# Attention weights of a hybrid streaming encoder: transposes by DMA instead of TensorE

## The chip, the core and the metric

One program on one core of a Trainium2 chip. The core has five engines, each with an instruction queue of its own that runs in order: TensorE (PE; its weight loads are listed apart as PEld), VectorE (DVE), ScalarE (ACT), GpSimd (POOL) and SyncE (SP), which here issues nearly all DMAs. Matrix products land in PSUM (eight banks of 128 x 512 f32); SBUF holds the rest. The metric is the device time of one execution in microseconds (us): the median before the change is 2810.27 us over three runs (2809.77 to 2811.77).

## The reference

One layer on x[1, 2048, 1024] in f32: a root-mean-square norm, one input projection whose columns feed three groups of heads (a diagonal state-space layer, differential attention with 6 heads, a gated linear recurrence called HGRN2), an output projection with residual, then a gated MLP with a causal convolution, and a last norm. The change lies in the attention:

```python
def attend(args):                      # one block of 128 queries
    q_blk, blk = args
    sc = jnp.einsum('bqhcd,bkhcd->bhcqk', q_blk, k).astype(jnp.float32) * scale
    ...
    bias = jnp.where(visible[None], -slopes[:, None, None] * dist[None], MASK_VALUE)
    p = jax.nn.softmax(sc + bias[None, :, None], axis=-1)
    w = p[:, :, 0] - lam * p[:, :, 1]
    return jnp.einsum('bhqk,bkhd->bqhd', w, v)
```

Each head has two softmax maps (c = 0, 1) that are joined into one matrix of weights w, which multiplies the values; each head's output is then normed. A block of queries sees the keys up to its own end.

## The kernel before

Products are made in f16 with values split in two: a high half, f16(a), and a low half, f16(a - high); three products (high high, high low, low high) stand for an f32 one.

The program is written as two streams of Python generators. `left` makes the projections and then the attention; `right` makes the state-space layer, HGRN2, the output projection and the MLP. `weave` joins them by weights, and a list scheduler with a timing model then sets the order of instructions on each engine at build time. On the chip each engine runs that order and waits on semaphores. SP's DMAs too go out in that order: a DMA that waits for an engine holds those behind it.

`phase_attn` runs twice: for query blocks 0 to 7 (keys up to 1024), and in its `lean` form for blocks 8 to 15 (keys up to 2048), each time over six heads, 96 blocks in all. One block i of a head, with L = 128 (i + 1) keys:

- Scores (L835): for both maps, products of 512 keys each into a PSUM tile t_ps (two buffers). DVE adds the distance bias and writes to t_sc, one f32 tile [128 queries, keys] for each map, with a running maximum t_mx (L839). t_sc has six buffers in the first form, four in the lean one, so three and two blocks in flight.
- t_nm, the exponents' offset (L844); exponentials by ACT in place with their sums t_la (L849); a ratio t_a (L854, L855); then DVE joins the maps in place, in pieces of 1024 keys (L861): t_sc[0] = t_sc[1] * t_a + t_sc[0].
- To the keys' side (L871 to L875): for each 512 keys, four f32 transposes on PE into the single PSUM buffer t_pt; ACT copies it twice, scaled by 16: as f32 to t_wf and as f16 to t_wt[:, 0]; POOL writes the difference to t_wt[:, 1].
- The product with the values (L883): for each 128 keys three matmuls of 64 columns into t_po, high high, high low, low high; ACT copies t_po to t_y and sums its squares (L887, L889).

After a head's eight blocks the norm's factors are made (L893 on, with a factor 1/16), and after every second head t_y is transposed through t_pt too (L910), split into t_yo and stored.

Beside the attention PE makes HGRN2's projections (g_pq, g_pv, both at L98) up to about 1000 us, a part of the output projection (o_pm, L1394), from 1225 us on the up products of the MLP's first half of the tokens (f_pm, L98), and at the end the first of its down products (f_pd, L1679). For half of the MLP's up weights, POOL makes sums (f_sum, L141), which ACT and DVE split into f_w (L54, L62), and SP stores them to Wd; the others are loaded from Wd (L150). After the attention come the second half's up products, and the down products of both.

Of the kernel before, what the change touches and what calls it, by code (L numbers as in the profile page):

```python
# [26 lines left out]
CH = 512  # L27
# [682 lines left out]
class AttnConst:  # L710


    def __init__(self, K, cp, lq1, lk1, lq2, lk2, subln_g):
        nc = K.nc
        V = nc.vector
        self.base = base = cp.tile([128, S], F32, name="t_base")
        nc.gpsimd.iota(base.bitcast(I32), pattern=[[-1, S]], base=S - 128, channel_multiplier=1)
        V.tensor_copy(base, base.bitcast(I32))
        V.scalar_tensor_tensor(
            out=base, in0=base, scalar=-1.0, in1=base, op0=ALU.mult, op1=ALU.min  # L720
        )
# [12 lines left out]
        self.nlam = nlam = cp.tile([128, 1], F32, name="t_nlam")
        V.tensor_tensor(out=nlam, in0=lexp[:, 1:2], in1=lexp[:, 0:1], op=ALU.subtract)
        V.tensor_scalar(out=nlam, in0=nlam, scalar1=-lam_init, scalar2=None, op0=ALU.add)
        self.lk = lk = cp.tile([128, 2], F32, name="t_lk")
        nc.gpsimd.memset(lk, 0.0)
        V.tensor_tensor(out=lk[:, 0:1], in0=lsum[:, 0:1], in1=lsum[:, 1:2], op=ALU.max)
        V.tensor_scalar(out=lk[:, 0:1], in0=lk[:, 0:1], scalar1=0.0, scalar2=None, op0=ALU.max)  # L740
        V.tensor_scalar(
            out=lk[:, 0:1], in0=lk[:, 0:1], scalar1=-1.0, scalar2=-math.log(2.0 + lam_init),
            op0=ALU.mult, op1=ALU.add,
        )
        self.gc = gc = cp.tile([128, 1], F32, name="t_gc")
        for e in range(2):
            nc.sync.dma_start(
                out=gc[64 * e:64 * e + 64, :], in_=subln_g[0].rearrange("(p o) -> p o", o=1)
            )
        V.tensor_scalar(  # L750
            out=gc, in0=gc, scalar1=(1.0 - lam_init) * YS, scalar2=None, op0=ALU.mult
        )


def phase_attn(K, A, QKd, Vd, Yd, i0, i1, s_bufs, lean):

    tc, nc = K.tc, K.nc  # L760
    V = nc.vector
    NT = i1 - i0
# [2 lines left out]
    with ExitStack() as es:  # L765
        kp = es.enter_context(tc.tile_pool(name="t_k", bufs=2, reuse_waits="tile"))
        sp = es.enter_context(tc.tile_pool(name="t_s", bufs=s_bufs, reuse_waits="tile"))
        wp = es.enter_context(tc.tile_pool(name="t_w", bufs=4 if lean else 5, reuse_waits="tile"))
        mp = es.enter_context(tc.tile_pool(name="t_m", bufs=3, reuse_waits="tile"))
        op = es.enter_context(tc.tile_pool(name="t_o", bufs=2, reuse_waits="tile"))  # L770
        ps_s = es.enter_context(tc.tile_pool(name="t_ps", bufs=2, reuse_waits="tile", space=PSUM))
        ps_t = es.enter_context(tc.tile_pool(name="t_pt", bufs=1, reuse_waits="tile", space=PSUM))
        ps_o = es.enter_context(tc.tile_pool(name="t_po", bufs=1, reuse_waits="tile", space=PSUM))
        fp = es.enter_context(tc.tile_pool(name="t_f", bufs=2 if lean else 3, reuse_waits="tile"))
        kq = {}

        def stack(a, i, parts, h, cols):
# [28 lines left out]
        for h in range(NH):  # L806
# [13 lines left out]
            for i in range(i0, i1):  # L820
# [27 lines left out]
                for c in range(2):  # L848
# [7 lines left out]
                    out=a[:, 1:2], in0=la[:, 0, n_:n_ + 1], scalar1=a[:, 0:1], scalar2=nlam[:, 0:1],  # L856
                    op0=ALU.mult, op1=ALU.mult,
                )
                for k0 in range(0, L, 1024):
                    k1 = min(L, k0 + 1024)  # L860
                    V.scalar_tensor_tensor(  # L861
                        out=sc[0][:, k0:k1], in0=sc[1][:, k0:k1], scalar=a[:, 1:2],
                        in1=sc[0][:, k0:k1], op0=ALU.mult, op1=ALU.add,
                    )
                wts = []
                for k in range(0, L, 512):
                    n = min(512, L - k)
                    wt = wp.tile([128, 2, 512], F16, tag="w", name="t_wt")
                    pt = ps_t.tile([128, 512], F32, tag="t", name="t_pt")
                    for b in range(0, n, 128):  # L870
                        nc.tensor.transpose(pt[:, b:b + 128], sc[0][:, k + b:k + b + 128], K.ident)  # L871
                    wf = fp.tile([128, 512], F32, tag="f", name="t_wf")
                    nc.scalar.activation(out=wf[:, 0:n], in_=pt[:, 0:n], func=AF.Copy, scale=16.0)  # L873
                    nc.scalar.activation(out=wt[:, 0, 0:n], in_=pt[:, 0:n], func=AF.Copy, scale=16.0)  # L874
                    nc.gpsimd.tensor_tensor(  # L875
                        out=wt[:, 1, 0:n], in0=wf[:, 0:n], in1=wt[:, 0, 0:n], op=ALU.subtract
                    )
                    wts.append(wt)
                po = ps_o.tile([128, HD], F32, tag="o", name="t_po")
                for b in range(i + 1):  # L880
                    cc = slice(128 * (b % 4), 128 * (b % 4) + 128)
                    for w, v in ((0, 0), (0, 1), (1, 0)):
                        nc.tensor.matmul(  # L883
                            out=po, lhsT=wts[b // 4][:, w, cc], rhs=vt[:, b, 64 * v:64 * v + 64],
                            start=(b == 0 and w + v == 0), stop=(b == i and w == 1),
                        )
                nc.scalar.copy(ot[:, n_, :], po)  # L887
                sq = mp.tile([128, HD], F32, tag="sq", name="t_sq")
                nc.scalar.activation(  # L889
# [2 lines left out]
                yield 2 * (i + 1) + 1  # L892
            s, v = [mp.tile([128, NT], F32, tag=f"e{j}", name=f"t_e{j}") for j in range(2)]  # L893
            V.reciprocal(out=s, in_=la[:, 0, :])
            V.tensor_scalar(out=s, in0=s, scalar1=1.0 / 16.0, scalar2=None, op0=ALU.mult)
            V.tensor_tensor(out=v, in0=s, in1=s, op=ALU.mult)
            V.tensor_tensor(out=v, in0=v, in1=ss, op=ALU.mult)
            V.tensor_scalar(
# [6 lines left out]
                op=ALU.mult,  # L905
            )
            for j in range(NT // 4 if e == 1 else 0):
                pt = ps_t.tile([128, 512], F32, tag="t", name="t_pt")
                for b in range(4):
                    nc.tensor.transpose(pt[:, 128 * b:128 * b + 128], y[:, 4 * j + b, :], K.ident)  # L910
                o = op.tile([128, 2, CH], F16, tag="yo", name="t_yo")
                K.split(o[:, 0, :], o[:, 1, :], pt, gc[:, 0:1])
                c0 = 128 * i0 + j * CH
                nc.sync.dma_start(out=Yd[2 + h // 2, :, :, c0:c0 + CH], in_=o)
# [413 lines left out]
def phase_tail(K, x, Xd, Yd, Ad, w_out, norm_g, W, conv_w, conv_b, w_down, final_g, out, es,  # L1328
# [472 lines left out]
    def activations(hc, half, pool, pm, few, st_n, w_n, a_n, behind):  # L1801

        wp, st = pool("f_w1", w_n), pool("f_st1", st_n)
        sm = pool("f_sm1", 2) if half == 0 else None
        tp, ap = pool("f_t1", 2), pool("f_a1", a_n)
        done = factors(ap, Ad[half])
        ts = [
# [217 lines left out]
```

## Time and profile before

| What | Value |
| --- | --- |
| Median of three runs | 2810.27 us |
| The profiled execution | 2806.09 us, its span 2804.4 us |
| Mean granted PE clock | 0.943 |
| The attention, first score to last product | 440 to about 1950 us |
| Transposes of the weights, PE | 816, 146.6 us |
| ACT's copies to t_wf | 240, 126.7 us (those to t_wt 127.1) |
| POOL's subtractions to t_wt | 240, 286.5 us |
| Joining of the maps, DVE | 144, 167.9 us |

A row of a group has the engine, operation, output <- inputs, shape and count, then the busy time in all, the mean of one in ns, and the idle time of the engine before it with what ended it. Instructions overlap on PE, so its busy time over the count is less than the mean.

### The profile page before, as it was taken

To read this page: it belongs to the slowest core of one execution; us is meant where nothing else is said; L and a number is where in the kernel's file an instruction comes from. 1 tells how busy PE (TensorE), PEld (TensorE's weight loads), DVE (VectorE), ACT (ScalarE), POOL (GpSimd) and SP (SyncE) were. 2 spreads that over 40 slices of the span, in tenths; PEclk is the share of its full clock that TensorE was granted. 3 is DMA by queue.
4 is the path that set the end of the run, shared out by engine and by line. 5 is a ranking of instruction groups with operands and counts; after the bars stand their busy time and mean duration, and the time that the engine had idled before them with its cause. 6 is when DMAs were issued, how large, how long until landed. Compare 5 with 4: busy or idle time off the path is not lost.

```text
span 2804.4 us, 44619 instructions
## 1 busy us (share of the span) xinstructions
PE 2528.7 (90%) x16254; PEld 1465.3 (52%) x16254; DVE 2008.0 (72%) x3904; ACT 1341.1 (48%) x2579; POOL 1347.2 (48%) x1191
## 2 busy tenths in 40 slices
PE   5998898989999998968898888879999999999998
PEld 3654546877777765444444444434444444444443
DVE  7566745788787887798888889885654855555565
ACT  5333344557665665676565456653134422222221
POOL 4788602334343443266566666642801444444180
PEclk8999998989989989989999999989999999999999
DMA  6675553232223225623444434357775655554733
GB/s 225 234 219 187 166 169 99 65 91 69 60 78 91 52 86 134 211 84 112 135 135 128 152 111 128 101 213 242 270 264 197 215 166 155 166 154 143 267 105 120
DMA packets 339500, 420.74 MB, mean 150 GB/s; under 512 B 61840, under 2 KB 217808, under 8 KB 338256
## 3 DMA queue, kind: packets, MB, share of 16 engines
q1 hardware_dynamic: 317104, 377.51, 42.8%
q10 hardware_dynamic: 22176, 40.38, 3.9%
q8 instruction: 128, 2.10, 0.3%
q14 instruction: 92, 0.75, 0.1%
HBM read 289.30 MB, written 127.93 MB: 149 GB/s over the span
## 4 chain that ended last, share of the span: by engine, by line
PE 41%; DVE 16%; issue 6%; ACT 4%; DMA 4%; POOL 4%; SPq 0%; ACTq 0%; DVEq 0%; POOLq 0%
PE f_pm L98 18%; PE f_pd L1679 10%; DVE t_sc L839 3%; PE o_pm L1394 3%; DVE t_sc L861 2%; PE g_pv L98 2%; PE g_pq L98 1%; ACT t_sc L849 1%; PE t_pt L871 1%; DVE f_t L1520 1%; PE t_ps L835 1%; DVE f_w L62 1%; DMA o_y<-Yd 1%; PE g_pl L1147 1%; PE t_po L883 1%
## 5 line engine op out<-in xcount | busy, mean ns | idle before, releaser
L98 PE MATMUL f_pm<-f_q,f_w 128*128 128x512 f16 x3696 | 857.8, 388 | 6.2 <-DVE rs_i L72 5.7
L98 PEld LDWEIGHTS <-f_w 128*128 128x128 f16 x3696 | 365.3, 100 | 493.7 <-issue 98.4
L875 POOL TENSOR_TENSOR t_wt<-t_wf,t_wt 128x512 f16<-128x512 f32 (+2 forms) x240 | 286.5, 1195 | 451.3 <-ACT t_wt L874 365.0
L1679 PE MATMUL f_pd<-f_dw,f_da 128*128 128x512 f16 x1848 | 406.9, 382 | 9.5 <-DMA f_da<-Ad 7.8
L1679 PEld LDWEIGHTS <-f_da 128*128 128x128 f16 x1848 | 181.3, 98 | 228.7 <-DMA f_da<-Ad 8.8
L849 ACT ACTIVATE t_sc<-t_sc,t_nm 128x128 f32<-128x128 f32 (+7 forms) x192 | 229.2, 1198 | 53.5 <-DVE t_nm L844 51.9
L835 PE MATMUL t_ps<-t_k,t_q 96*128 96x512 f16 (+2 forms) x480 | 170.0, 369 | 83.7 <-DVE t_mx L839 80.5
L839 DVE CUSTOM_DVE_ANT_0 t_sc<-t_ps,t_base,t_mx 128x512 f32<-128x512 f32 (+3 forms) x288 | 185.2, 643 | 36.4 <-PE t_ps L835 29.6
L873 ACT ACTIVATE t_wf<-t_pt 128x512 f32<-128x512 f32 (+2 forms) x240 | 126.7, 528 | 132.9 <-PE t_pt L871 96.1
L883 PE MATMUL t_po<-t_v,t_wt 128*128 128x64 f16 x2448 | 145.5, 198 | 37.1 <-POOL t_wt L875 32.4
L883 PEld LDWEIGHTS <-t_wt 128*128 128x128 f16 x2448 | 124.8, 101 | 94.3 <-POOL t_wt L875 48.0
L861 DVE SCALAR_TENSOR_TENSOR t_sc<-t_sc,t_a 128x1024 f32<-128x1024 f32 (+7 forms) x144 | 167.9, 1193 | 1.6
L98 PE MATMUL g_pq<-g_h,g_w 128*128 128x256 f16 x1152 | 157.3, 291 | 9.9 <-DVE g_sg L1069 7.3
L60 DVE TENSOR_TENSOR f_a<-f_t,f_a 128x512 f16<-128x512 f32 x132 | 134.8, 1027 | 39.6 <-ACT f_a L54 36.1
L98 PE MATMUL g_pv<-g_w,g_h 128*128 128x256 f16 x1152 | 151.1, 284 | 12.0 <-ACT g_w L54 8.0
L1744 POOL TENSOR_TENSOR f_k<-f_k,f_k 128x512 f32<-128x512 f32 x88 | 126.1, 1433 | 73.1 <-ACT f_k L1776 65.9
L871 PE MATMUL t_pt<-ident,t_sc 128*128 128x128 f32 x816 | 146.6, 296 | 14.6 <-ACT t_wt L874 9.4
L1744 POOL TENSOR_TENSOR f_db<-f_db 128x1536 f32<-128x1536 f32 (+1 forms) x32 | 129.2, 4073 | 61.0 <-DMA f_db<-in_w_down_dram 61.0
L1744 POOL TENSOR_TENSOR f_t<-f_t,f_t 128x512 f32<-128x512 f32 x66 | 104.3, 1594 | 108.5 <-ACT f_a L54 85.4
L1394 PE MATMUL o_pm<-o_w,o_y 128*128 128x512 f16 x624 | 145.0, 388 | 10.0 <-DMA o_y<-Yd 9.6
L54 ACT ACTIVATE f_a<-f_t 128x512 f16<-128x512 f32 x154 | 95.9, 629 | 118.1 <-POOL f_t L1744 54.9
L62 DVE SCALAR_TENSOR_TENSOR f_dw<-f_db,f_dw 128x1536 f16<-128x1536 f32 (+1 forms) x36 | 104.0, 2904 | 55.2 <-ACT f_dw L54 55.2
(328 smaller groups left out, 4856.5 us busy)
## 6 DMA issues: line engine op xcount, KB each, us to landing
f_w<-Wd SPq DMA_DIRECT2D x231, 256.0 KB, 2.7
Wd<-f_w SPq DMA_DIRECT2D x154, 256.0 KB, 2.1
Ad<-f_a ACTq DMA_DIRECT2D x154, 256.0 KB, 2.3
f_da<-Ad SPq DMA_DIRECT2D x42, 768.0 KB, 4.5
g_h<-Hd SPq DMA_DIRECT2D x24, 1024.0 KB, 6.5
f_db<-in_w_down_dram SPq DMA_DIRECT2D x24, 768.0 KB, 8.7
o_wst<-in_w_out_dram SPq DMA_DIRECT2D x32, 512.0 KB, 5.8
o_y<-Yd SPq DMA_DIRECT2D x52, 256.0 KB, 4.9
```

The costliest lines, as they stand in the source:

```text
L60: nc.vector.tensor_tensor(out=lo, in0=src, in1=hi, op=ALU.subtract)
L98: nc.tensor.matmul(out=out, lhsT=lhs(a, k), rhs=rhs(b, k), start=(n == 0), stop=(n == 3 * nk - 1))
L835: nc.tensor.matmul(out=ps[:, 0:k1 - k0], lhsT=qt[:, c, 128 * (i % 4):128 * (i % 4) + 128], rhs=kt[:, c, k0:k1], start=True, stop=True,)
L839: V.tensor_tensor_reduce(out=sc[c][:, k0:k1], in0=ps[:, 0:k1 - k0], in1=bs[:, k0:k1], scale=1.0, scalar=-3e38 if j == 0 else mx[:, c, j - ...
L849: nc.scalar.activation(out=sc[c][:, 0:L], in_=sc[c][:, 0:L], func=AF.Exp, scale=SLOPES[h], bias=nm[:, c:c + 1], accum_out=la[:, c, n_:n_ + 1],
L861: V.scalar_tensor_tensor(out=sc[0][:, k0:k1], in0=sc[1][:, k0:k1], scalar=a[:, 1:2], in1=sc[0][:, k0:k1], op0=ALU.mult, op1=ALU.add,)
L871: nc.tensor.transpose(pt[:, b:b + 128], sc[0][:, k + b:k + b + 128], K.ident)
L875: nc.gpsimd.tensor_tensor(out=wt[:, 1, 0:n], in0=wf[:, 0:n], in1=wt[:, 0, 0:n], op=ALU.subtract)
L883: nc.tensor.matmul(out=po, lhsT=wts[b // 4][:, w, cc], rhs=vt[:, b, 64 * v:64 * v + 64], start=(b == 0 and w + v == 0), stop=(b == i and w ...
L1394: nc.tensor.matmul(out=ps[t], lhsT=y[:, k, a, 128 * t:128 * t + 128], rhs=w[:, b, k, :], start=(q == qs[0] and i == 0), stop=(q == qs[-1] ...
L1679: nc.tensor.matmul(out=ps[t], lhsT=a[:, q, x, tk], rhs=w[:, y, q, :], start=(first and q + x + y == 0), stop=(last and q == n - 1 and y == 1),
L1744: eng.tensor_tensor(out=o, in0=a, in1=b, op=op)
```

## The change

The joined weights are no longer transposed by PE. ACT casts t_sc[0] to f16 into `hl`, a view in f16 of t_sc[1], which is done with by then; its first half of columns holds the high halves. POOL writes the low halves, t_sc[0] - high, to its second half. Then two DMA transposes on SP's queue (high, then low) write all of the block's keys to one tile t_wt [128 keys, 2, blocks, 128 queries]. The matmuls with the values now take all high halves first, then the low ones.

The factor 16 moves into the exponents: log 16 is added to t_lk once, and the 1/16 of the norm goes. The buffers change: t_wt has 3 (lean 2) of a whole block instead of 5 (4) of 512 keys; t_wf and t_pt are gone, t_ps has three banks instead of two and serves the transposes of t_y too; t_yo has one buffer instead of two. In the MLP's first half the pool f_sm1 (f_sum) has one buffer instead of two.

```diff
+        V.tensor_scalar(out=lk, in0=lk, scalar1=math.log(16.0), scalar2=None, op0=ALU.add)
...
-        wp = es.enter_context(tc.tile_pool(name="t_w", bufs=4 if lean else 5, reuse_waits="tile"))
+        wp = es.enter_context(tc.tile_pool(name="t_w", bufs=2 if lean else 3, reuse_waits="tile"))
...
-        ps_s = es.enter_context(tc.tile_pool(name="t_ps", bufs=2, reuse_waits="tile", space=PSUM))
-        ps_t = es.enter_context(tc.tile_pool(name="t_pt", bufs=1, reuse_waits="tile", space=PSUM))
+        ps_s = es.enter_context(tc.tile_pool(name="t_ps", bufs=3, reuse_waits="tile", space=PSUM))
...
-        fp = es.enter_context(tc.tile_pool(name="t_f", bufs=2 if lean else 3, reuse_waits="tile"))
...
+                hl = sc[1].bitcast(F16)
...
-                wts = []
-                for k in range(0, L, 512):
-                    n = min(512, L - k)
-                    wt = wp.tile([128, 2, 512], F16, tag="w", name="t_wt")
-                    pt = ps_t.tile([128, 512], F32, tag="t", name="t_pt")
-                    for b in range(0, n, 128):
-                        nc.tensor.transpose(pt[:, b:b + 128], sc[0][:, k + b:k + b + 128], K.ident)
-                    wf = fp.tile([128, 512], F32, tag="f", name="t_wf")
-                    nc.scalar.activation(out=wf[:, 0:n], in_=pt[:, 0:n], func=AF.Copy, scale=16.0)
-                    nc.scalar.activation(out=wt[:, 0, 0:n], in_=pt[:, 0:n], func=AF.Copy, scale=16.0)
+                for k0 in range(0, L, 1024):
+                    k1 = min(L, k0 + 1024)
+                    nc.scalar.copy(hl[:, k0:k1], sc[0][:, k0:k1])
                     nc.gpsimd.tensor_tensor(
-                        out=wt[:, 1, 0:n], in0=wf[:, 0:n], in1=wt[:, 0, 0:n], op=ALU.subtract
+                        out=hl[:, LM + k0:LM + k1], in0=sc[0][:, k0:k1], in1=hl[:, k0:k1],
+                        op=ALU.subtract,
                     )
-                    wts.append(wt)
+                wt = wp.tile([128, 2, i1, 128], F16, tag="w", name="t_wt")
+                for w in range(2):
+                    nc.sync.dma_start_transpose(
+                        out=wt[:, w, 0:i + 1, :], in_=hl[:, LM * w:LM * w + L]
+                    )
                 po = ps_o.tile([128, HD], F32, tag="o", name="t_po")
-                for b in range(i + 1):
-                    cc = slice(128 * (b % 4), 128 * (b % 4) + 128)
-                    for w, v in ((0, 0), (0, 1), (1, 0)):
...
+                for w in range(2):
+                    for b in range(i + 1):
+                        for v in range(2 - w):
+                            nc.tensor.matmul(
+                                out=po, lhsT=wt[:, w, b, :], rhs=vt[:, b, 64 * v:64 * v + 64],
...
-            V.tensor_scalar(out=s, in0=s, scalar1=1.0 / 16.0, scalar2=None, op0=ALU.mult)
...
-                pt = ps_t.tile([128, 512], F32, tag="t", name="t_pt")
+                pt = ps_s.tile([128, 512], F32, tag="s", name="t_pt")
...
-        sm = pool("f_sm1", 2) if half == 0 else None
+        sm = pool("f_sm1", 1) if half == 0 else None
```

The scheduler orders the whole program anew, on all engines. Two places show it. On ACT, in the first head of the lean form beside HGRN2 (names with g_), before:

```order
L849 ACTIVATE t_sc,t_la<-t_sc,t_nm 128x1664 x2
L1244 ACTIVATE g_sq<-g_y 128x512
L873 ACTIVATE t_wf<-t_pt 128x512
L874 ACTIVATE t_wt<-t_pt 128x512
L1136 ACTIVATE g_d<-g_d 128x512
L873 ACTIVATE t_wf<-t_pt 128x512
L874 ACTIVATE t_wt<-t_pt 128x512
L1053 ACTIVATE g_x<-g_pq 128x2x256
L873 ACTIVATE t_wf<-t_pt 128x512
L874 ACTIVATE t_wt<-t_pt 128x512
L887 COPY t_y<-t_po 128x64
```

The same place in the changed program:

```order
L849 ACTIVATE t_sc,t_la<-t_sc,t_nm 128x1664 x2
L1063 ACTIVATE g_vn<-g_pv 128x256
L1064 ACTIVATE g_sg<-g_pv 128x256
L1242 ACTIVATE g_sq<-g_y 128x512
L886 COPY t_y<-t_po 128x64
L888 ACTIVATE t_sq,t_ss<-t_po 128x64
L1134 ACTIVATE g_d<-g_d 128x512
L868 CAST t_sc<-t_sc 128x1024
L868 CAST t_sc<-t_sc 128x640
L1051 ACTIVATE g_x<-g_pq 128x2x256
```

Pairs of copies out of PSUM, one pair for every 512 keys, have become two casts inside t_sc for the whole block. On SP, in a later head of the lean form beside the MLP's up products (f_w and Wd are the up weights, f_wst their raw form, t_k and t_q the next head's keys and queries), before:

```order
L150 DMA f_w<-Wd_93 128x1024
L145 DMA Wd_92<-f_w 128x1024
L150 DMA f_w<-Wd_93 128x1024
L779 DMA t_k<-QKd 32x2x2048 x3
L779 DMA t_q<-QKd 32x2x512 x3
L150 DMA f_w<-Wd_93 128x1024 x5
L145 DMA Wd_94<-f_w 128x1024 x4
```

In the changed program, where it loads a head's keys beside the same weights:

```order
L875 DMA_TRANSPOSE t_wt<-t_sc 128x15x128
L150 DMA f_w<-Wd_91 128x1024 x3
L875 DMA_TRANSPOSE t_wt<-t_sc 128x15x128
L145 DMA Wd_92<-f_w 128x1024 x3
L779 DMA t_k<-QKd 32x2x2048 x3
L779 DMA t_q<-QKd 32x2x512 x3
L145 DMA Wd_92<-f_w 128x1024 x3
L875 DMA_TRANSPOSE t_wt<-t_sc 128x16x128
L129 DMA f_wst<-in_w_up_dram 128x8x128
L150 DMA f_w<-Wd_93 128x1024 x3
L145 DMA Wd_92<-f_w 128x1024
L875 DMA_TRANSPOSE t_wt<-t_sc 128x16x128
```

Between its first and its last transpose SP issues 192 of them and 426 other DMAs, each behind the waits of those ahead of it. On PE the transposes are gone from between the matmuls; 231 matmuls of f_pd that stood before the attention's last product with values stand behind it.

More of the change, by code (lines that the diff above doesn't have):

```diff
@@ L875, in phase_attn @@
                     nc.gpsimd.tensor_tensor(
-                        out=wt[:, 1, 0:n], in0=wf[:, 0:n], in1=wt[:, 0, 0:n], op=ALU.subtract
-                    )
-                    wts.append(wt)
-                po = ps_o.tile([128, HD], F32, tag="o", name="t_po")
-                for b in range(i + 1):
-                    cc = slice(128 * (b % 4), 128 * (b % 4) + 128)
-                    for w, v in ((0, 0), (0, 1), (1, 0)):
[L883 to L886, printed above, removed]
+                        out=hl[:, LM + k0:LM + k1], in0=sc[0][:, k0:k1], in1=hl[:, k0:k1],
@@ new lines, in phase_attn @@
+                        op=ALU.subtract,
+                    )
+                wt = wp.tile([128, 2, i1, 128], F16, tag="w", name="t_wt")
[3 more added lines that the diff above has]
+                    )
+                po = ps_o.tile([128, HD], F32, tag="o", name="t_po")
+                for w in range(2):
[3 more added lines that the diff above has]
+                                out=po, lhsT=wt[:, w, b, :], rhs=vt[:, b, 64 * v:64 * v + 64],
+                                start=(b == 0 and w + v == 0), stop=(b == i and w == 1),
+                            )
@@ L907, in phase_attn @@
             for j in range(NT // 4 if e == 1 else 0):
-                pt = ps_t.tile([128, 512], F32, tag="t", name="t_pt")
+                pt = ps_s.tile([128, 512], F32, tag="s", name="t_pt")
                 for b in range(4):
                     nc.tensor.transpose(pt[:, 128 * b:128 * b + 128], y[:, 4 * j + b, :], K.ident)
-                o = op.tile([128, 2, CH], F16, tag="yo", name="t_yo")
+                o = op.tile([128, 2, CH], F16, tag="yo", bufs=1, name="t_yo")
                 K.split(o[:, 0, :], o[:, 1, :], pt, gc[:, 0:1])
```

## The prediction

> **What bounds the kernel now.** First the head of the page, busy time by engine:
>
> ```profile
> span 2804.4 us, 44619 instructions
> PE 2528.7 (90%) x16254; PEld 1465.3 (52%) x16254; DVE 2008.0 (72%) x3904; ACT 1341.1 (48%) x2579; POOL 1347.2 (48%) x1191
> ```
>
> TensorE (PE) is first, but that is a mean. The view of busy time by window, cut where the attention starts (440 us), changes to its long blocks (883), where the feed-forward products begin (1225) and where the attention ends (1950), says more. Columns: length, busy time of PE, its weight loads, DVE, ACT, POOL, then clock and DMA.
>
> ```profile
> 440.00:883.00 443.00, 403.48 (x4039) 332.95 (x4038) 338.20 (x1013) 268.63 (x683) 165.88 (x177) 0.93 0.28 77
> 883.00:1225.00 342.00, 304.63 (x2580) 208.28 (x2578) 278.83 (x682) 223.39 (x430) 136.18 (x121) 0.91 0.39 116
> 1225.00:1950.00 725.00, 629.58 (x3773) 314.92 (x3772) 615.18 (x965) 427.31 (x765) 440.33 (x310) 0.92 0.42 137
> 1950.00:2804.40 854.40, 828.05 (x3840) 377.21 (x3838) 496.62 (x669) 249.78 (x410) 353.60 (x198) 0.99 0.57 187
> 1200.00:1300.00 100.00, 74.79 (x505) 42.98 (x505) 92.94 (x158) 66.39 (x126) 71.30 (x50) 0.84 0.26 78
> ```
>
> In the first stage PE is busy 91.1% and DVE 76.3%; in the second 89.1% and 81.5%; in the third 86.8% and 84.9%: **two engines share the bound there**. The last row, one 100 us window, shows that DVE can reach 93%. After 1950 PE is at 96.9%, and nothing of the change lies there. What PE and DVE wait for in the attention, from the waits between 440 and 1950 (us, times, longest):
>
> ```profile
> PE t_ps L835 <- DVE t_mx L839: 80.5, 76, 4.6
> PE t_po L883 <- POOL t_wt L875: 32.4, 31, 5.8
> DVE t_a L854 <- ACT t_sc L849: 53.8, 39, 3.9
> DVE t_sc L839 <- PE t_ps L835: 49.6, 45, 4.5
> ```
>
> PE waits most for a score bank that DVE has not emptied, then for the split's low half; DVE waits for ACT's exponentials and for scores.
>
> **What goes from PE.** The 816 transposes of the weights. Same windows, the tile t_sc alone (first busy column PE, third DVE, fourth ACT):
>
> ```profile
> 440.00:883.00 443.00, 41.47 (x220) 26.45 (x220) 133.29 (x205) 80.58 (x196) 0.93 0.28 77
> 883.00:1225.00 342.00, 44.09 (x246) 30.98 (x246) 144.78 (x186) 69.45 (x84) 0.91 0.39 116
> 1225.00:1950.00 725.00, 61.04 (x351) 43.73 (x350) 192.80 (x234) 87.97 (x104) 0.92 0.42 137
> ```
>
> PE loses 41.5 + 44.1 + 61.0 = 146.6 us and keeps 362.0, 260.5 and 568.5. DVE loses only twelve tiny instructions. So in the second and third stage DVE, with 278.8 and 615.2, becomes the longer one. The sum must go by it.
>
> **What moves between ACT, POOL and DMA.** By form (us in all, mean ns), with two rows of the same shape as the new instructions:
>
> ```profile
> L874 ACT ACTIVATE t_wt<-t_pt 128x512 f16<-128x512 f32 x168 | 99.7, 594 | 0.0
> L873 ACT ACTIVATE t_wf<-t_pt x240: 252/587/644, 449.4 to 1926.6; 128x512 f32<-128x512 f32 x96, 128x128 f32<-128x128 f32 x12, 128x384 f32<-128x384 f32 x12
> L54 ACT ACTIVATE o_w<-o_wst 128x1024 f16<-128x1024 f32 x26 | 27.3, 1052 | 49.5 <-PE o_pm L1394 27.2 <-DMA o_wst<-in_w_out_dram 22.3
> L58 POOL TENSOR_TENSOR a_w<-a_wst,a_w 128x1024 f16<-128x1024 f32 x9 | 20.3, 2267 | 0.2
> ```
>
> ACT drops 336 copies of 512 columns at about 0.59 us and 144 narrower ones, gains 60 casts of 1024 at 1.05 us and 84 shorter ones at no more than that: over 100 us less on an engine at 59 to 65%. It shortens DVE's wait for exponentials; I give it no term of its own. POOL subtracts the same elements in 144 pieces rather than 240, at 2.27 us for 1024: no dearer. Its output is now f16 inside t_sc, so t_sc[1] is held until the low half's transpose has landed.
>
> The 192 DMA transposes, 32 KB for each 128 x 128 block, 1632 blocks, 53 MB, have no row. The nearest, KB and median us to landing, and the issue on SP (ns):
>
> ```profile
> Wd<-f_w SPq DMA_DIRECT2D x154, 256.0 KB, 2.1
> Vd<-a_vo SPq DMA_DIRECT2D x16, 192.0 KB, 3.8
> t_v<-Vd SPq DMA_DIRECT2D x6, 512.0 KB, 4.1
> f_db<-in_w_down_dram SPq DMA_DIRECT2D x8, 512.0 KB, 10.9
> L799 SPq DMA_DIRECT2D t_v<-Vd x12: 319/344/773, 433.1 to 1508.7; - x12
> ```
>
> Ends: 2.1 and 10.9 us. A transpose reads and writes short pieces, and the nearest row is the store of Vd, whose runs have 256 bytes: above the floor of 2.1 us it takes 1.7 us for 192 KB. A long block has 12.5 x 32 = 400 KB in each half: 2.1 + 3.5 = 5.6 us, which I take. For the queue: DMA engines are busy 28 to 42% of these stages; at 1.7 us for 192 KB, 53 MB are 460 us, 0.30 of the attention's 1510: it fits. SP pays 192 x 0.34 = 66 us at the low end and, if held until each landing, 192 x 5.6 = 1075 at the high end; I take the low end and name the rest below.
>
> A rule of the Trainium skill bears on the amount: "DMA: Bandwidth & Descriptors", Latency and other measured facts, gives an effective 261 GB/s to DMA transposes; by it, an estimate, 53 MB are 205 us. No row here shows a transpose.
>
> **Is the trip covered?** A block of 13 x 128 keys, the middle of the long ones, from its last score product, by form:
>
> ```profile
> L839 DVE CUSTOM_DVE_ANT_0 t_sc<-t_ps,t_base,t_mx 128x128 f32<-128x128 f32 x36 | 12.4, 344 | 5.2 <-PE t_ps L835 4.4
> L844 DVE SCALAR_TENSOR_TENSOR t_nm<-t_mx,t_lk 128x2 f32<-128x2 f32 x96 | 34.3, 357 | 0.7
> L849 ACT ACTIVATE t_sc<-t_sc,t_nm 128x1664 f32<-128x1664 f32 x12 | 20.1, 1678 | 6.8 <-DVE t_nm L844 6.7
> L855 DVE TENSOR_SCALAR t_a<-t_la,t_a,t_nlam 128x1 f32<-128x1 f32 x96 | 25.9, 270 | 1.4
> L854 DVE RECIPROCAL t_a<-t_la 128x1 f32<-128x1 f32 x96 | 15.2, 159 | 54.2 <-ACT t_sc L849 53.8
> L861 DVE SCALAR_TENSOR_TENSOR t_sc<-t_sc,t_a 128x1024 f32<-128x1024 f32 x60 | 87.6, 1467 | 0.8
> L861 DVE SCALAR_TENSOR_TENSOR t_sc<-t_sc,t_a 128x640 f32<-128x640 f32 x12 | 14.3, 1190 | 0.0
> L98 PE MATMUL f_pm<-f_q,f_w 128*128 128x512 f16 x3696 | 857.8, 388 | 6.2 <-DVE rs_i L72 5.7
> ```
>
> High half: 0.34 + 0.36 + 2 x 1.68 + 0.16 + 0.27 + 1.47 + 1.19, then a cast of 640 (0.7): issued at 7.8 us, landed at 13.4. Low half: POOL starts after the first cast (7.0), takes 2.27 + 1.5, issued at 10.8, landed at 16.4 us. These hold no queueing. On PE, counting the rows between a long block's last score product and its first product with values and pricing each at busy over count (857.8 / 3696 = 0.232 us for f_pm), the order of the changed program leaves 20.0 us of PE work in the mean of 48 blocks (34.6 before); at the 80% that PE is busy there by the sum below, that is 25 us. So the trip is covered with about 9 us for queueing, and I cost the wait at nothing; POOL's 32.4 us of wait may stay as it is.
>
> **Other edits.** The third score bank eases the 80.5 and 49.6 us of waits above: that is what lets DVE go up. The smaller f_sm1 (one buffer) makes each POOL sum of the made weights wait for DVE's split of the one before:
>
> ```profile
> POOL f_sum L141 <- DVE f_w L62: 37.9, 29, 3.7
> ```
>
> All 55 sums waiting as these do (1.3 us) would add 34 us to POOL, which idles 285 us in that stage: nothing, unless POOL falls behind. And 231 down products that stood before the last t_po on PE now stand after it:
>
> ```profile
> L1679 PE MATMUL f_pd<-f_dw,f_da 128*128 128x512 f16 x1848 | 406.9, 382 | 9.5 <-DMA f_da<-Ad 7.8
> L1657 DVE SCALAR_TENSOR_TENSOR f_r<-f_pd,f_r x112: 673/679/693, 1904.2 to 2796.2; 128x512 f32<-128x512 f32 x112
> ```
>
> 231 x 0.220 = 50.9 us of PE that used to fill gaps, 52.5 at 96.9% behind; they take 14 x 0.68 = 9.5 us of DVE along, 10.4 of its stage.
>
> **The sum.** Stage one goes by PE at its present 91.1%: 362.0 / 0.911 = 397.4, -45.6. The others by DVE, which I put at 91% (76 to 85 now, 93 at best; banks, ACT and POOL are freer): 278.8 / 0.91 = 306.4, -35.6; 615.2 / 0.91 = 676.0, -49.0. The moved products +52.5 - 10.4. In all -88 us, from the profiled execution's 2806.1 (span 2804.4 and 1.7 around it) to 2718; the median of the runs lies 4 higher, so **2722**.
>
> **Rivals.** (1) PE stays the bound and DVE gives more: all 146.6 us and half of the 80.5 us of bank waits go, 2623. For it: those waits; against: DVE would need 97% of the attention's time. Chance 0.13, from 2600 to 2680.
> (2) DVE is the bound already and rises no further than 84.9%: 278.8 / 0.849 = 328.4, -13.6; third stage 0; first -45.6; +42: -17, 2793. The transposes were then hidden. For it: DVE's 85% against PE's 87%; against: DVE's own waits. Chance 0.20, a quarter of it within 0.2%, which is about what a measurement of this kernel can tell from no change.
> (3) **Slower: t_po waits for the low half.** If transposes land like f_db, and the low one queues behind the high one, it lands at 7.8 + 2 x 10.9 = 29.6 us against 25 of cover: 4.6 us for each of 48 long blocks, 221 us, 2943. It decides from 88 / 48 = 1.8 us beyond the cover. It is worse for the SP queue: behind a transpose waiting for POOL stand the loads of f_w and the stores of Wd. For it: only two pairs of t_sc in the long stage, DVE's queueing, cover cut from 34.6 to 20.0; against: t_v's 4.1 us for the same bytes. Chance 0.22.
> (4) The 128-blocks go one at a time, each a landing of 2.1 us: 1632 x 2.1 = 3427 us where the attention has 1510, so some 4720. Against it: t_v moves sixteen such columns of blocks in 4.1 us. Chance 0.03.
>
> Beside it, the Trainium skill's "VectorE: DVE Perf Modes", The three transpose paths, speaks against this change: 390 ns for a 128 x 128 block on TensorE, 1309 by DMA, TensorE where PSUM serves. One after the other, an estimate, 1632 x 1.309 is 2136 us, which would be rival four.
>
> **How the numbers follow.** Forecast 0.42 (2680 to 2775), rivals 0.13, 0.20, 0.22, 0.03. Faster 0.42 + 0.13 + 0.15 = 0.70, same 0.05, slower 0.25. The range runs from the middle of rival one, 2640, to where half of rival three is in, 2880; about 0.17 is left out.
>
> **What would show it.** After: no t_pt of t_sc; DVE near 91% from 883 on; PE's wait on t_mx well under 80 us; t_wt landing in 3 to 6 us. Wrong: t_po waiting on DMA t_wt for more than 90 us in all (rival three), or DVE near 85% (two). If SP's loads of f_w come late, f_pm shows waits that it has not now.

## The result and the profile after

The changed kernel takes **2843.52 us** in the median of four runs (2835.14 to 2844.76) beside 2810.02 us of the kernel before on the same chip: a ratio of 1.0113, 95% interval 1.0092 to 1.0133. It is slower by 33 us where the prediction said 88 us faster. The time lies in the predicted range, but the sign is wrong. Of all the runs below, one of x14, at 4114 us, was in a slower state of the chip and is left out of x14's ratio. Head of the page of the changed kernel, with its granted clock by slice and its main DMA queue:

```profile
span 2842.4 us, 42776 instructions
PE 2453.8 (86%) x15438; PEld 1381.2 (49%) x15438; DVE 2001.4 (70%) x3893; ACT 1224.4 (43%) x2231; POOL 1320.1 (46%) x1095
PEclk8999998988888898888999999979899999999999
q1 hardware_dynamic: 532144, 431.02, 53.4%
```

PE's busy time falls by 75 us only, though transposes of 146.6 us are gone. In the trace of the kernel before, PE is busy with transposes and with no other matmul for only 75.4 us (21.1, 24.4 and 29.9 in the prediction's three stages); for the rest of the 146.6 they overlap other matmuls. The granted clock is lower too (0.924 in the mean, 0.943 before). Busy time by window, cut at 880 us, at the first f_pm and at the last t_po:

```profile
440.00:880.00 440.00, 383.90 (x3689) 307.16 (x3687) 339.54 (x1018) 247.03 (x595) 162.28 (x152) 0.88 0.51 110
880.00:1268.00 388.00, 317.99 (x2774) 208.42 (x2773) 330.46 (x785) 217.58 (x377) 157.33 (x106) 0.86 0.67 162
1268.00:1886.00 618.00, 492.78 (x2806) 227.91 (x2804) 535.90 (x786) 315.62 (x521) 390.50 (x249) 0.92 0.54 155
1886.00:2842.00 956.00, 901.42 (x4157) 409.18 (x4154) 517.68 (x728) 272.50 (x445) 358.34 (x204) 0.97 0.57 188
```

PE is at 87% in the first window, not at 91%, and its clock there is 0.88 instead of 0.93. DVE reaches 87% in the third (535.9 of 618), not 91%. The DMA share is 0.51, 0.67 and 0.54 in the first three windows, beside 0.28, 0.39 and 0.42 in the prediction's three stages. Yet the attention itself ends 47 us earlier (last t_po 1886.0, before 1932.7). All of that, and 38 us more in this execution, is lost in the other stream. Its milestones, from the view by tile:

| First or last start, us | before | after |
| --- | --- | --- |
| last g_pq (HGRN2) | 994.1 | 1024.6 |
| first f_pm | 1225.1 | 1267.9 |
| first f_pd | 1869.8 | 1892.7 |
| last t_po (attention) | 1932.7 | 1886.0 |
| last f_pd | 2795.8 | 2833.8 |

What PE waits for, from the waits of the whole span, and the transposes on SP with their landing, from the view by tile (durations in ns, min/median/max):

```profile
PE t_po L882 <- DMA t_wt<-t_sc: 77.7, 34, 18.6
PE t_ps L835 <- DVE t_mx L839: 75.1, 70, 10.4
PE f_pd L1677 <- ACT f_dw L54: 29.9, 3, 14.4
PE f_pm L98 <- DVE f_w L62: 13.6, 10, 4.4
L875 SPq DMA_TRANSPOSE t_wt<-t_sc x192: 1124/1382/6152, 450.1 to 1879.6; - x192
DMA to landing us min/median/max: 2.2/3.7/8.9
```

The transposes land sooner than estimated (3.7 us in the median of all, not 5.6), but each holds SP for 1.4 us in the median and for up to 6.2. The durations of the 192 add up to 330.7 us in the trace. PE's largest wait is now for them, 77.7 us: the obvious suspect, and the wrong one.

### The profile page after: what moved, and what is told of

It is laid out like the page before. It is cut to its first block, busy times and chain, and to the rows that moved or that the text cites. A ratio compares the mean times of both kernels' runs of the same rounds, so it can differ in the third digit from the quotient of the medians.

```text
span 2842.4 us, 42776 instructions
## 1 busy us (share of the span) xinstructions
PE 2453.8 (86%) x15438; PEld 1381.2 (49%) x15438; DVE 2001.4 (70%) x3893; ACT 1224.4 (43%) x2231; POOL 1320.1 (46%) x1095
## 2 busy tenths in 40 slices
DMA packets 554533, 474.13 MB, mean 167 GB/s; under 512 B 276880, under 2 KB 432848, under 8 KB 553296
## 5 line engine op out<-in xcount | busy, mean ns | idle before, releaser
L98 PE MATMUL f_pm<-f_q,f_w 128*128 128x512 f16 x3696 | 841.5, 387 | 38.6 <-DVE f_w L62 13.6
L1677 PE MATMUL f_pd<-f_dw,f_da 128*128 128x512 f16 x1848 | 406.6, 383 | 31.7 <-ACT f_dw L54 29.9
L869 POOL TENSOR_TENSOR t_sc<-t_sc 128x1024 f16<-128x1024 f32 (+7 forms) x144 | 247.8, 1732 | 323.8 <-ACT t_sc L868 299.2
L849 ACT ACTIVATE t_sc<-t_sc,t_nm 128x128 f32<-128x128 f32 (+7 forms) x192 | 229.0, 1194 | 93.3 <-DVE t_nm L844 86.8
L835 PE MATMUL t_ps<-t_k,t_q 96*128 96x512 f16 (+2 forms) x480 | 160.0, 371 | 78.8 <-DVE t_mx L839 75.1
L882 PE MATMUL t_po<-t_v,t_wt 128*128 128x64 f16 x2448 | 109.7, 202 | 83.8 <-DMA t_wt<-t_sc 77.7
L60 DVE TENSOR_TENSOR f_a<-f_t,f_a 128x512 f16<-128x512 f32 x132 | 148.0, 1128 | 47.4 <-ACT f_a L54 43.4
L98 PE MATMUL g_pq<-g_h,g_w 128*128 128x256 f16 x1152 | 163.2, 304 | 12.1 <-DVE g_sg L1067 10.0
L98 PE MATMUL g_pv<-g_w,g_h 128*128 128x256 f16 x1152 | 155.4, 291 | 12.8 <-ACT g_w L54 7.7
L882 PEld LDWEIGHTS <-t_wt 128*128 128x128 f16 x2448 | 98.6, 104 | 123.2 <-DMA t_wt<-t_sc 99.5
L1742 POOL TENSOR_TENSOR f_k<-f_k,f_k 128x512 f32<-128x512 f32 x88 | 127.3, 1446 | 67.1 <-ACT f_k L1774 64.9
L839 DVE CUSTOM_DVE_ANT_0 t_sc<-t_ps,t_base 128x512 f32<-128x512 f32 (+2 forms) x192 | 120.7, 632 | 40.3 <-DMA t_wt<-t_sc 16.3
L98 PEld LDWEIGHTS <-g_w 128*128 128x128 f16 x1152 | 123.5, 109 | 47.0 <-issue 16.3
L54 ACT ACTIVATE f_w<-f_sum 128x512 f16<-128x512 f32 x110 | 69.1, 628 | 176.5 <-DVE f_sum L141 74.4
```

Of the source, the lines that this page charges most:

```text
L54: nc.scalar.activation(out=hi, in_=src, func=AF.Copy, scale=scale)
L60: nc.vector.tensor_tensor(out=lo, in0=src, in1=hi, op=ALU.subtract)
L98: nc.tensor.matmul(out=out, lhsT=lhs(a, k), rhs=rhs(b, k), start=(n == 0), stop=(n == 3 * nk - 1))
L835: nc.tensor.matmul(out=ps[:, 0:k1 - k0], lhsT=qt[:, c, 128 * (i % 4):128 * (i % 4) + 128], rhs=kt[:, c, k0:k1], start=True, stop=True,)
L839: V.tensor_tensor_reduce(out=sc[c][:, k0:k1], in0=ps[:, 0:k1 - k0], in1=bs[:, k0:k1], scale=1.0, scalar=-3e38 if j == 0 else mx[:, c, j - ...
L849: nc.scalar.activation(out=sc[c][:, 0:L], in_=sc[c][:, 0:L], func=AF.Exp, scale=SLOPES[h], bias=nm[:, c:c + 1], accum_out=la[:, c, n_:n_ + 1],
```

## The experiments

Each variant is a new plan of the whole program. x9 below differs from the kernel before by two buffers and came out 7 us from it, so I read nothing into single differences under about 7 us. Each ratio is to the kernel before on the same chip; the variants ran on five chips, so where ratios and medians disagree on the difference of two variants, I give both.

| Run | us | ratio to before, 95% | first f_pd |
| --- | --- | --- | --- |
| x1 no transposes | 2809.08 | 0.999 (0.9978 to 1.0003) | 1859.8 |
| x2 transposes beside | 2843.8 | 1.0121 (1.0104 to 1.0138) | 1896.6 |
| x3 PE work back | 2884.34 | 1.0263 (1.0246 to 1.0279) | 1923.2 |
| x4 plain copies | 2817.94 | 1.0027 (1.0014 to 1.0041) | 1869.2 |
| x5 attention later | 2832.2 | 1.0073 (1.0058 to 1.0088) | 1868.9 |
| x6 later in both | 2882.54 | 1.0253 (1.0237 to 1.0269) | 1864.4 |
| x7 on ACT | 2952.96 | 1.0513 (1.0469 to 1.0556) | 1993.8 |
| x8 before, fewer buffers | 2845.45 | 1.0121 (1.0104 to 1.0137) | 1892.0 |
| x9 before, cut and padded | 2817.53 | 1.002 (1.0007 to 1.0033) | 1868.1 |
| x10 place given back | 2822.25 | 1.0038 (1.0025 to 1.0052) | 1867.3 |
| x11 copies in three | 2837.42 | 1.0079 (1.0054 to 1.0104) | 1886.6 |
| x12 one transpose | 2832.03 | 1.0061 (1.0043 to 1.0079) | 1875.5 |
| x13 short blocks only | 2822.06 | 1.0045 (1.003 to 1.006) | 1866.4 |
| x14 long blocks only | 2835.62 | 1.0083 (1.0057 to 1.0108) | 1881.4 |
| x15 none, and place | 2782.37 | 0.9898 (0.9876 to 0.9919) | 1833.3 |
| x16 place and one transpose | 2822.75 | 1.0042 (1.0026 to 1.0059) | 1860.0 |
| x17 long blocks and place | 2824.98 | 1.0049 (1.0034 to 1.0064) | 1870.4 |
| x18 the same, later | 2809.83 | 0.9993 (0.9979 to 1.0007) | 1853.6 |

The last column comes first. But for x6, every span ends 934 to 963 us after the first down product starts, wherever the attention ends (1838 us in x15, 1986 in x7). So the end goes with the right stream's start into f_pd more than with the end of the attention.

### Is it the wait for the transposes?

Theory A says that t_po's wait is the loss, B that the order puts the attention ahead of the stream that ends last, C that SP and the queues are held.

x1:

```diff
-                    nc.sync.dma_start_transpose(...)
...
-                                out=po, lhsT=wt[:, w, b, :], ...
+                                out=po, lhsT=hl[:, LM * w + 128 * b:LM * w + 128 * b + 128], ...
```

> Left out: the DMA transposes. The products with the values read the cast halves untransposed (128 x 128 blocks of hl, same shapes, same count, still behind ACT's cast and POOL's subtraction). Theory A (the trip: t_po waits 77.7 us on PE for the transposes, and that wait is the loss): t_po waits for POOL only, 2843 - 78 = about 2765, below the kernel before. Theory B (the order: attention runs ahead of the stream that ends the program, and the stalls are where nothing else is planned): at most 15 us better, 2828 to 2850. Theory C (SP and the queues: the transposes hold SP 1.4 us each and load the DMA engines): as low as A, but only here and not in the run that keeps the transposes beside.

x2 has the second part of that edit alone; the DMAs stay.

> As x1, but the two DMA transposes of each block are issued too, into t_wt, which nobody reads. Theory A: as x1, about 2765, since nothing waits for them. Theory B: 2828 to 2850. Theory C: stays near 2843, some 50 to 80 us above x1, with f_pm's wait on f_w as long as in the changed kernel (13.6 us DVE f_w, 38.6 us idle before f_pm).

x2 settles it: PE waits for no transpose any more, and the time is that of the changed kernel (2843.8 and 2843.5). The waits of x2:

```profile
PE t_ps L835 <- DVE t_mx L839: 88.4, 86, 7.6
PE f_pd L1677 <- ACT f_dw L54: 29.0, 3, 17.9
PE t_po L882 <- POOL t_sc L869: 27.9, 29, 1.9
PE t_po L882 <- ACT t_sc L868: 26.7, 20, 8.4
```

In x1 the last two rows, t_po's waits for the two halves, are 12.8 and 36.3 us: t_po waits about as long in both runs, and they differ by 35 us. **Theory A falls.** Issuing the transposes costs those 35 us though no product waits for one (only DVE waits, 13.0 us, for the t_sc that they read). x1 came out at the kernel before, 19 us under the least that B allowed, and 44 us over what A and C said: most of the 33 us come with the DMAs, as C said, though C asked for 50 to 80. Why PE's freed time gives nothing even in x1 stayed open until x15.

x4 and x11 ask whether it is SP's time or the bytes.

```diff
-                    nc.sync.dma_start_transpose(
-                        out=wt[:, w, 0:i + 1, :], in_=hl[:, LM * w:LM * w + L]
+                    nc.sync.dma_start(                      # x11: three, partitions 0:48, 48:96, 96:128
+                        out=wt[:, w, 0:i + 1, :],
+                        in_=hl[:, LM * w:LM * w + L].rearrange("p (b q) -> p b q", q=128),
```

> The two DMA transposes of a block as plain DMA copies of the same bytes into the same t_wt (so the weights stay untransposed). SP is held some 0.4 us a DMA instead of 1.4. Theory A: landing 2 to 3 us instead of 3.7, t_po's wait on DMA under 40 us, about 2800. Theory B: within 15 us of 2843. Theory C by SP's time: about x1; by the bytes alone: about x2.

> x4 (plain copies in place of the transposes, 2818 us) with each copy in three by partitions (48, 48, 32): 576 DMAs, which at 0.47 us hold SP for 271 us, as long as the 192 transposes do (1.4 us each), with the bytes of x4. If the transposes cost by SP's time: 2835 to 2850, as the changed kernel. If they cost by what they do to the DMA engines (packets under 512 B 66448 in x4, 276880 in the changed kernel): 2813 to 2825.

The first row is of x4, by tile, then two rows of x4's waits; behind them x11's issues and landing:

```profile
L875 SPq DMA_DIRECT2D t_wt<-t_sc x192: 464/471/2175, 448.4 to 1862.0; - x192
```

```profile
PE t_ps L835 <- DVE t_mx L839: 80.8, 63, 5.6
PE t_po L883 <- DMA t_wt<-t_sc: 57.8, 30, 14.0
```

```profile
L876 SPq DMA_DIRECT2D t_wt<-t_sc x576: 503/585/2738, 449.4 to 1876.8; - x192
DMA to landing us min/median/max: 1.7/2.5/9.1
```

The same bytes as 192 copies (0.47 us on SP each in the median, 109.2 us in all) cost 9 us over x1, though t_po waits 57.8 us for them. Cut in three, with the same bytes and quick landings but SP held for 353.4 us in all, they cost 25 us over x1 by the ratios, 28 by the medians. So **SP's time is worth about 15 to 20 us**. That is not the number of DMAs: the 192 transposes of x2 hold SP about as long (341.6 us) and cost even 6 to 12 us more than x11. Nor is it the waiting at the head of SP's queue, for x4's copies stand there too, behind the same halves, and cost 9. Whether the last 6 to 12 us are the transposes' small packets (276880 under 512 B, x4 66448) is not decided.

x12 and x7 try to relieve SP.

```diff
+                nc.sync.dma_start_transpose(out=wt[:, 0:2 * i + 2, :], in_=hl[:, 0:2 * L])   # x12
...
+                    nc.scalar.dma_start_transpose(                                           # x7
```

> The changed kernel with one transpose a block: the low halves lie right behind the high ones (at L instead of LM) and one DMA of 2 L columns brings both, so 96 instead of 192. If the hold on SP is per DMA (1.12 us the shortest, 1.22 the median of short blocks, 1.5 of long ones): SP is held some 130 us less, and if SP's time is what costs, 2820 to 2835. If the cost is by bytes and packets: 2838 to 2848. If t_po's wait for the high half counts after all, since it now waits for POOL too: above 2850.

> The changed kernel with the 192 transposes issued by ACT instead of SP, order otherwise planned anew. Theory C in its form by SP (each transpose holds SP 1.4 us, some 290 us in all, and waits at the head of its queue for ACT and POOL, so loads come late): about x4, 2810 to 2825, unless ACT's own 290 us hurt. In its form by traffic (276880 packets under 512 B instead of 61840, DMA share 53% instead of 43%): 2835 to 2855.

```profile
L874 SPq DMA_TRANSPOSE t_wt<-t_sc x96: 1180/3242/9754, 450.6 to 1858.5; - x96
```

That row is x12's. One transpose of twice the columns holds SP 3.2 us in the median, and the 96 hold it 312.9 us in all, where the 192 held it 330.7: joining hardly shortens the hold. So x12's time lies in the range of a shorter hold by luck. What gave its 11 us is not shown, and x16 below does not repeat them. x7 missed both of its ranges: with the transposes on ACT, whose work HGRN2 needs too, the last g_pq moves to 1105.7 us, and t_po's waits on DMA grow to 185.0 us.

### Two kilobytes: the place of f_dst

x8 was meant as a control of the cut buffers.

```diff
-        sm = pool("f_sm1", 2) if half == 0 else None
+        sm = pool("f_sm1", 1) if half == 0 else None
...
+                o = op.tile([128, 2, CH], F16, tag="yo", bufs=1, name="t_yo")
```

> The kernel before with the change's two cut buffers alone: f_sm1 one instead of two, t_yo one instead of two. If the cuts cost nothing, as the prediction had it: 2803 to 2818. If POOL's wait for f_w (37.9 to 65.1 us in the changed kernel) reaches PE: 2820 to 2845, and then the transposes are not all of the loss.

The kernel before with nothing but these two cuts is as slow as the changed one: 2845.45. POOL's wait for f_w grew from 37.9 to 47.1 us only, and stays at 48.3 in x9 below, where most of the loss is gone. The loss sits behind the up products. SP's waits between 1820 and 1900 us, first row x8, then the kernel before; and the loads of f_dst with the last f_a of each, by tile:

```profile
SPq L1612 <- DVE f_a L60: 32.7, 1, 32.7
```

```profile
SPq L1612 <- DVE f_dw L62: 30.5, 11, 14.1
```

```profile
L1612 SPq DMA_DIRECT2D f_dst<-in_w_down_dram x42: 327/379/1261, 1887.1 to 2243.4; - x42
L60 DVE TENSOR_TENSOR f_a<-f_t,f_a x21: 677/687/1791, 1698.4 to 1885.4; 128x512 f16<-128x512 f32 x21
```

```profile
L1612 SPq DMA_DIRECT2D f_dst<-in_w_down_dram x42: 327/378/1223, 1837.3 to 2203.4; - x42
L60 DVE TENSOR_TENSOR f_a<-f_t,f_a x19: 677/1128/1752, 1700.3 to 1885.8; 128x512 f16<-128x512 f32 x19
```

In the kernel before, the first down weights are loaded 48 us ahead of the last f_a. In x8 the load waits for it. The reason is in the memory of the built programs. These are the places of the buffers, in bytes of a partition:

```
f_dst, in all programs:           139776-143872, 143872-147968, 147968-152064
f_t0, with f_sm1 of two buffers:  131584-135680, 135680-139776
f_t0, with f_sm1 of one buffer:   133632-137728, 137728-141824
```

The MLP's pools are a stack; with f_sm1 smaller by 2 KB all behind it moves up, and f_t0, from which the last f_a is made, reaches over the first buffer of f_dst (theory D). x9 keeps one buffer for f_sum but fills the place:

```diff
+            gap = sm.tile([128, CH], F32, tag="gap", name="f_gap")
```

> x8 (the kernel before with f_sm1 and t_yo at one buffer each) plus one unused tile of 2 KB in f_sm1, so that the addresses of the MLP's later tiles are those of the kernel before, while f_sum still has one buffer. Theory D (place: with f_sm1 2 KB smaller the last buffer of f_t0 reaches over the first buffer of f_dst, so the first down weights are loaded only when the last f_a is read off, at 1887 instead of 1837 us): 2805 to 2818. Rival (number: POOL's sums wait for the single buffer, 47 to 65 us on f_w): 2835 to 2850, as x8.

28 of x8's 34 us come back (2817.53), and f_dst goes out at 1843.5 again, 32 us before the last f_a. **Place, not number.** x10 gives the place back to the changed kernel:

```diff
+        sm = pool("f_sm1", 2) if half == 0 else None
...
+            yield from activations(hc, 0, pooler(e1), pm, 1, 3, 5, 2, None)
```

> The changed kernel with f_sm1 at two buffers again, which its memory allows with f_a1 at two instead of three: f_t0 ends below f_dst again. Theory D: the first load of f_dst goes out 20 us or more before the last f_a, and the 34 us of x8 come back: 2800 to 2820. If place matters only in the kernel before, or a third f_a1 buffer is worth as much: 2835 to 2855.

2822.25: 21 us back, of the 34 that were expected. First load and last f_a in x10 and, second fence, in the changed kernel:

```profile
L1610 SPq DMA_DIRECT2D f_dst<-in_w_down_dram x42: 327/379/1284, 1840.4 to 2223.9; - x42
L60 DVE TENSOR_TENSOR f_a<-f_t,f_a x22: 676/1282/2608, 1700.7 to 1884.0; 128x512 f16<-128x512 f32 x22
```

```profile
L1610 SPq DMA_DIRECT2D f_dst<-in_w_down_dram x42: 327/378/1265, 1887.0 to 2239.8; - x42
L60 DVE TENSOR_TENSOR f_a<-f_t,f_a x22: 677/1226/2603, 1712.3 to 1883.6; 128x512 f16<-128x512 f32 x22
```

### What PE's time is worth

> The changed kernel with 816 f32 transposes of t_sc[0] on PE put back (same count, shape and 4 per bank) into one PSUM bank that nobody reads; t_ps has two banks again. If PE is the bound in the attention (what the prediction said of the first stage), they cost up to 147 us: 2920 to 2990. If PE has nothing to give (theories A and B: PE waits in any case), most of it falls into idle time: 2843 to 2875. If the lower granted clock is what costs (fewer stalls, higher clock), 2810 to 2843.

```diff
+                    nc.tensor.transpose(pt[:, k % 512:k % 512 + 128], sc[0][:, k:k + 128], K.ident)
```

41 us more than the changed kernel, above what A and B allowed, and far below 147 (with two score banks instead of three, so not by the transposes alone). PE's busy time rose by 79 us, to 2532.9, not by 147: put back, the transposes again overlap other matmuls. The granted clock rose from 0.924 to 0.936, and the time did not fall. So the clock alone does not explain the loss.

x15 is x1 with x10's place.

> x1 (no transposes at all, the cast halves read untransposed) with the place of f_dst given back as in x10. If place and SP's hold are all that stands against the freed PE time: 2809 - 21 = 2788, give or take 8, that is 22 us under the kernel before. If the freed time is lost in the order anyway: 2800 to 2812.

2782.37, 29 us under the kernel before and some 26 below x1: what the freed PE time and the other edits give when neither the transposes nor the place take it back. Its windows:

```profile
440.00:880.00 440.00, 393.19 (x3887) 317.43 (x3884) 354.63 (x1046) 253.32 (x611) 166.65 (x156) 0.89 0.28 76
880.00:1236.00 356.00, 297.81 (x2531) 193.42 (x2531) 307.15 (x740) 203.63 (x352) 147.18 (x102) 0.86 0.40 118
1236.00:1838.00 602.00, 504.42 (x2850) 232.37 (x2849) 534.21 (x806) 321.96 (x534) 394.21 (x249) 0.91 0.40 134
1838.00:2781.00 943.00, 894.71 (x4150) 406.75 (x4148) 518.39 (x726) 269.86 (x441) 357.12 (x205) 0.98 0.57 188
```

The attention ends at 1838, 94 us earlier than before, with DVE at 86% and 89% in its later windows. But 943 us follow where 872 did: 71 us are given back. PE's busy time there is 894.7 us, 49 more than the 845.4 after the last t_po of the kernel before, for 223 more matmuls; the other 22 us are idle time.

x5 and x6 shift work under the attention by the weave's weights (0.62 to 0.66; 0.44 to 0.60 and 0.62 to 0.70).

```diff
-LW = [6.0, 0.44, 5.0, 2.5, 0.62, 1.0]
+LW = [6.0, 0.44, 5.0, 2.5, 0.66, 1.0]
```

> The changed kernel with one number of the weave changed: the long blocks' weight 0.62 to 0.66 (LW[4]), so that the attention is spread over more of the right stream: 392 of the first 924 down products (f_pd) stand before its last t_po in the order, where the changed kernel has none and the kernel before has 231. Theory B (the freed PE time is given back behind the attention, where the chain f_dst, f_dw has nothing beside it: PE idle 29.9 us before f_pd and a PE at 63% from 1860 to 1900 us): 30 to 60 us better, 2783 to 2813. Theory C (SP held by the transposes) alone: 2833 to 2853.

> As x5 with both weights raised: 0.44 to 0.60 (short blocks) and 0.62 to 0.70 (long ones); 528 down products before the last t_po, 528 up products after 72 blocks where the changed kernel has 0. Theory B: HGRN2 and f_pm start earlier as well (1024.6 and 1267.9 us in the changed kernel, 994.1 and 1225.1 before): 10 to 30 us below x5, 2760 to 2800. Theory C alone: 2833 to 2853. If the attention now ends too late to feed the second half: slower than x5.

x5 gained 11 us, a third of the least that B asked for. x6 lost 39: the attention ended at 2029.9 us, and new waits came behind it. From x6's waits:

```profile
PE f_pd L1677 <- ACT f_dw L54: 36.5, 2, 36.1
PE o_pm L1392 <- ACT o_w L54: 23.9, 3, 19.0
```

### Stage by stage, and both repairs

In x13 and x14 one form of the attention keeps the old path:

```diff
+                if not lean:      # x14, x17 and x18: if lean
+                    hl = sc[1].bitcast(F16)
...
+                else:
+                    wts = []
...
```

> DMA transposes in the first form alone (query blocks 0 to 7, 216 of the 816 blocks of 128 keys but 96 of the 192 DMAs); the long blocks as in the kernel before, with all of its buffers, so that f_sm1 keeps two and f_t0 ends below f_dst. If the first stage is where PE bounds (the prediction's 45.6 us there, less SP's hold in a stage with few loads on it): 2775 to 2800, faster than both. If the gain there is lost at once (HGRN2's last g_pq late as in the changed kernel, 1024.6 instead of 994 us): 2805 to 2825.

> DMA transposes in the lean form alone (blocks 8 to 15, 600 of the 816), the rest of the buffers as in the changed kernel (f_sm1 at one, so the place of f_dst is the changed kernel's). If SP's hold costs where the MLP's loads are queued and the place costs its 21 to 35 us: 2825 to 2845. If the short blocks were what made the changed kernel slow: 2800 to 2815.

> x10 and x12 together: f_dst's place given back, and one transpose a block. If they add up (21 and 11 us): 2808 to 2816, level with the kernel before. If x12's gain came from a chance of the planning: 2818 to 2828.

> x14 (DMA transposes in the long blocks alone) with f_dst's place given back as in x10. If the losses add up: 2836 - 21 = 2815, between 2805 and 2820, level with the kernel before. If the place is worth nothing here: 2830 to 2842.

> x17 with the long blocks' weight 0.62 raised to 0.65, so that 308 of the first 924 down products stand before the attention's last t_po (45 in x17, 231 in the kernel before). If the products exposed behind the attention are what keeps the freed PE time from showing: 15 to 30 us under x17, 2785 to 2803, faster than both kernels. If SP's hold or DVE take it back within the attention: within 8 us of x17.

x13 shows that the first stage's gain does not reach the end: with f_dst's place kept, DMA transposes of the short blocks alone make the kernel 13 us slower. Their last t_po comes at 807.4 us, 39 earlier than before, but the last g_pq at 1021.3, 27 later, as in the changed kernel: the attention runs ahead of the stream that ends last. Its first window has PE at 87% again, at a clock of 0.88:

```profile
440.00:880.00 440.00, 383.16 (x3698) 308.40 (x3696) 336.07 (x1019) 249.14 (x600) 162.82 (x154) 0.88 0.48 107
```

x14 is 23 us slower than before. x17, with the place, is 14 slower, between its two ranges: the place is worth 10 us here, not 21, so the parts do not simply add up. x16 equals x10. x18, with the products spread as far as 308 of them under the attention, gains 15 us and stands level with the kernel before. No version that transposes the weights by DMA beat it.

## Why the prediction was wrong

Three terms failed. The gain of 88 us was 29 (x15). The transposes, which had no term, cost 39. The cut buffer, put at nothing, cost 21.

- **"The smaller f_sm1 ... nothing, unless POOL falls behind."** I priced the buffer's waits, and these were not the cost. The cut cost 21 us by moving f_t0 over f_dst (x10; 34 with t_yo's cut in the kernel before, 28 of it by place, x8 and x9). A row could have raised the question: f_dst's loads began 48 us before the last f_a.
- **"SP pays 192 x 0.34 = 66 us at the low end ... I take the low end."** SP is held 330.7 us, five times that. In all the transposes cost 35 to 40 us (x2 less x1; x10 less x15), about 15 to 20 of them by SP's time (x11 less x4); what the rest is stays open. The prediction named the loads behind them, but under the rival in which t_po waits. The sign that it gave for late loads came: PE idles 38.6 us before f_pm, against 6.2 before.
- **"PE loses 41.5 + 44.1 + 61.0 = 146.6 us and keeps 362.0, 260.5 and 568.5."** This took a group's busy time off the engine's, though the group overlaps others. PE had the transposes alone for 75.4 us, so it keeps 382.4, 280.2 and 599.7. Then PE, not DVE, is the longer one in the second stage. At PE's present shares (91.1, 89.1 and 86.8%) the three stages give 23, 27 and 34 us, an estimate of some 85 in place of 130.
- **"Stage one goes by PE at its present 91.1% ... The others by DVE, which I put at 91%."** Without any transposes (x15) the attention ended 94 us earlier, not 130. PE stood at 89% in the first window (393.2 of 440) and DVE at 89% at best. (Rival one's 97% for DVE holds for the second and third stage; over the whole attention its sum gives 93%.) Part of the first stage's loss may be clock: 0.88 and 0.89 against 0.93, and a g_pq product between 440 and 1040 us took 303 and 299 ns in the mean against 289. The Trainium skill's "TensorE: Matmul & The Clock Gate", Part 1, has the gate follow how busy PE is. In the first window the traces agree, with fewer matmuls and a lower clock; in the third PE's share fell from 87 to 80% at the same 0.92. What the clock alone costs was not isolated.
- **"The moved products +52.5 - 10.4."** The mechanism was right, the size too small: in x15 71 us come back behind the attention. 49 of them are moved matmuls, as priced; the other 22 are idle time, and the chain to f_dw, bare there, makes PE wait 22.7 us.
- **"I cost the wait at nothing."** Right in the time, though the cover did not hold: 77.7 us of waits, and x2, without them, is no faster. Rival three asked for more than 90 us of them and a time of 2943; it did not happen, so the slower result is not its confirmation. Rival two's mechanism, DVE that rises no further, was nearest for the third stage (87%).
- **Landing 5.6 us:** 3.7 measured, 4.1 in the median for the last long blocks (9 to 16 blocks of 128 keys each, 1500 to 1890 us, by tile: `DMA to landing us min/median/max: 3.2/4.1/8.0`). Rival four is refuted with it. The Trainium skill's "VectorE: DVE Perf Modes", The three transpose paths, gives 1309 ns a block by DMA; here transposes of nine and more blocks land in 4.1 us, and the measurement decides.
- **The third score bank** was to ease 80.5 us of waits; 75.1 are left, 67.1 in x15.
- **POOL no dearer:** right, 247.8 us instead of 286.5. ACT's 100 us less had no term, and no run shows it alone.

The sum as measured, by the ratios times 2810: -29 for the freed PE and what came back (x15), +39 for the transposes (from x15 to x10), +21 for the place (from x10 to the changed kernel). Steps from one variant to the next must add up to the whole, so that they do proves nothing; in another order they differ (from x1 to x15 the place is worth 26).

## What to carry to other kernels

A buffer that is cut to make room moves everything stacked behind it: look at which later loads then lie over tiles that are freed late, not only at who waits for the cut buffer. A DMA transpose is paid for on the queue of the engine that issues it, for as long as it holds that queue; if that queue feeds the stream that ends last, a wait that looks large elsewhere may be free while the hold is not. When instructions overlap, a group's busy time is not what the engine gets back without it: count the time in which the group runs alone. Taking work off a nearly busy engine shortens the kernel only as far as the stream that ends last can start earlier: follow its milestones, not the busy share.

## What the runs showed of the hardware

A DMA transpose held SP 1.12 us at the least and 1.38 in the median: 1.21 for the short blocks alone (x13), 1.55 for the long ones (x14), and 3.24 for twice the columns (x12). A plain copy of the same bytes took 0.47. ACT as issuer was held as long (1.30 in the median in x7).

Where the 816 transposes of 16254 PE matmuls were gone, the others got a lower clock. Between 440 and 880 us it was 0.88 instead of 0.93. One form at a time shows the same: x13, which takes only the short blocks' transposes off PE, has 0.88 there and 0.93 from 880 to 1225 us; x14, which takes only the long blocks' off, has 0.92 and 0.86. With all of them put back on PE (x3) it was 0.91 in both.
